# One hybrid S5 / attention / SSD step: attention of each head pair woven with the next pair's products, modulation of layer 0 on TensorE

## The chip, the cores and the metric

The kernel runs on one core of one Trainium2 chip. The metric is device time in microseconds (us) from one launch to its end. TensorE (PE) multiplies, VectorE (DVE), ScalarE (ACT) and GpSimd (POOL) work element by element, SyncE (SP) issues almost all transfers. Each engine takes its own instructions in order.

## The reference

Two trunk layers run over 512 latent tokens and 128 context tokens, 1024 channels each, in float32. The change touches layer 0 only. What it computes:

```
sh, sc, gt, shf, scf, gtf = split(silu(cond) @ ada_w + ada_b, 6)     # for c and for c_ctx
h    = rmsnorm(x) * (1 + sc) + sh
proj = h @ w_in                              # 1024 -> 512 (S5 input) + 512 q + 512 k + 512 v
y_s5 = s5(proj[:512]);  y_s5 = gelu(y_s5) * sigmoid(gelu(y_s5) @ w_glu)
       # bidirectional linear recurrence, 32 groups of 16 channels, 64 complex states
attn = 8 heads of 64; latent queries see an 8 x 16 window with a bias table plus 128 cached
       keys in one softmax, context queries see the context
x    = x + gt * (concat(y_s5, attn) @ w_out)
x    = x + gtf * swiglu(rmsnorm(x) * (1 + scf) + shf)
```

The keys and values of the context tokens and the final S5 states are outputs too. Layer 1 (a Mamba-2 mixer and its feed-forward part) follows, and a last norm.

## The kernel before

**Layout and products.** Channels lie on the 128 partitions, the 640 tokens along the free dimension. A product with float32 weights is done in three passes: weights and inputs are each split into a high and a low part of type fp32r (`split`: ScalarE copies the high part, VectorE subtracts), and TensorE sums hi x hi, hi x lo, lo x hi. `gemm` (line 294) does 8 x 3 x 2 = 48 matmuls of 320 columns for one 128-wide output tile. The mixer's input projection has 16 such products: m = 0 to 3 give the S5 input `uT`, and for each head pair p the products 4 + p, 8 + p and 12 + p give q, k and v (`qkv`, three steps of a generator).

**Order.** Instructions are written by Python generators that yield between steps; a driver takes steps of several of them in turn ("weaves" them). The order of the text is a priority; a planner with a cost model of its own then fixes the order on each engine, allots the buffers and puts in the waits. `behind(engine)` keeps what a block holds behind the last instruction of that engine. Buffers come from an arena of 12 blocks (`blk`, 10 KB a partition) and 2 large ones (`big`); weights have 3 slots each for `whi` and `wlo`, 2 for `wraw`. PSUM has 4 one-bank tiles (`pm`) and 2 two-bank tiles (`acc`).

**Modulation.** One of layer 0's 48 modulation tiles (128 outputs, two conditions) is computed in one of two ways. `ada_rows` streams the weights through TensorE with the condition as a stationary operand of 2 columns, 512 outputs a matmul, and transposes the row back. `ada_tile` (line 248) has the weights transposed in DRAM and lets VectorE multiply and sum them with the condition spread over all partitions, one instruction for each of the two conditions. At the start, `ada_rows` makes tiles 0 to 11 (shift, first half of scale) and `ada_tile` tiles 12 to 15. Tiles 24 to 28 come in the S5 stage (`adae`), 29 to 39 in `ada_fill` during the later q, k, v products and attention, 16 to 23 in the output projection (`ada`), 40 to 47 and layer 1 in the feed-forward part.

**S5.** Input and output maps are built from the parameters (`s5_params`, `s5_input_maps`, `s5_output_maps`) by VectorE, GpSimd and TensorE. `s5_scan` runs 63 steps: backward on GpSimd, forward on VectorE (`mt`, `s5x`). The first 16 steps have four operations, the others three, each needing the one before. `s5_out` then makes the outputs in four blocks, and `glu` four products.

**Attention of a pair** (`attention(p)`, 13 steps) works on five query blocks: scores on TensorE, bias and row minimum in one VectorE reduction (line 1267), Exp on ScalarE, reciprocal and scaling on VectorE (line 1271), transposes (line 1278), products with the values (line 1291) into one `acc` tile that is held to the end.

**The order around the change.** `even_mixer` does all four pairs' q, k, v first, with four scan steps to each product; pairs 0 to 2 are written to DRAM (`qd`). Then attention(3) is woven with the rest of the scan; `qkv_back` reads a pair back before its attention; attention(0) has modulation tiles and the first steps of `s5_out`, attention(1) and (2) the rest of `s5_out` and `glu`. Each attention writes its output split into `ah`, `al`. The output projection (`ev_w_out`, eight products) follows in `build`, each with one modulation tile, the residual and the next norm's tile.

Of the kernel before, what the change touches and what calls it, by code (L numbers as in the profile page):

```python
# [16 lines left out]
NS, NP = 512, 128  # L17
# [47 lines left out]
def lay_out(a):  # L65
# [9 lines left out]
    d["ada_w"] = np.ascontiguousarray(a["ada_w"].transpose(0, 2, 1).reshape(96, 128, 1024)[12:])  # L75
# [45 lines left out]
class Kernel:  # L121
# [43 lines left out]
    def load_consts(self):  # L165
        self.nc.sync.dma_start(self.ident, self.I["ident"])
        self.nc.sync.dma_start(self.vecs, self.I["vecs"])
        self.condf = self.const.tile([128, 8, 2], F32, name="condf")
        self.nc.sync.dma_start(self.condf, self.I["cond_f"])
        self.nc.scalar.activation(self.condf, self.condf, AF.Silu)  # L170
# [18 lines left out]
    def load_cond(self):  # L189
        nc = self.nc  # L190
        self.condr = self.blk("condr", [BLK])[:1]
        nc.sync.dma_start(self.condr[:, :2048], self.I["cond"])
        nc.vector.memset(self.condr[:, 2048:2176], 1.0)

    def spread_cond(self):
        nc = self.nc
        self.cond = self.blk("cond", [2, 1024])
        cond = self.cond.rearrange("p s n -> p (s n)")
        for i in range(4):
            ps = self.psum()  # L200
            nc.tensor.matmul(ps, self.condr[:, 2048:2176], self.condr[:, i * 512:i * 512 + 512], start=True, stop=True)
            with self.behind(nc.scalar):
                nc.scalar.activation(cond[:, i * 512:i * 512 + 512], ps, AF.Silu)

    def ada_stage(self):
        nc, I = self.nc, self.I
        slot = lambda n: self.wpool.tile([128, 8, 128], F32, name=n, **({"bufs": 2} if n == "wraw" else {})).rearrange("p k m -> p (k m)")
        def rows(src, o, tiles):
            for i, b in enumerate(tiles):
                for j in range(0, 4, 1):  # L210
                    nc.sync.dma_start(b[:, j:j + 1], I[src][4 * i + j:4 * i + j + 1, :, o:o + 512].rearrange("k p n -> p k n"))
            return [b[:, j] for b in tiles for j in range(4)]

        self.sck = rows("ada_sc", 0, [self.blk("adak", [4, 512]) for _ in range(2)])
        self.scw = [slot("whi" if i % 2 else "wlo") for i in range(4)]
        for i in range(4):
            nc.sync.dma_start(self.scw[i], I["ada_w"][i])
        self.shk = rows("ada_sh", 0, [self.blk("adak", [4, 512]) for _ in range(2)])
        large = self.big("adab", [8, 512])
        self.w0 = self.raw_w(I["ev_w_in"][0], 8)  # L220
        self.shl = rows("ada_sh", 512, [large[:, :4], large[:, 4:]])

    def ada_rows(self, w, at):
        nc = self.nc
        n = w[0].shape[-1] // 512
        acc = self.mm.tile([128, 2, 512], F32, name="acc")
        ps = [acc[:, h] for h in range(n)]
        for k in range(8):
            for h in range(n):
                nc.tensor.matmul(ps[h][:2], self.condf[:, k], w[k][:, h * 512:h * 512 + 512], start=k == 0, stop=k == 7)  # L230
            yield
        row = self.blk("adar", [1024])[:2]
        for h in range(n):
            nc.scalar.activation(row[:, h * 512:h * 512 + 512], ps[h][:2], AF.Copy)
        pt = self.psum()
        for j in range(4 * n):
            nc.tensor.transpose(pt[:, 2 * j:2 * j + 2], row[:, j * 128:j * 128 + 128], self.ident[:2, :2])
        b = self.vec("ada_b")[:, at:at + 4 * n]
        nc.vector.tensor_tensor(self.mod[0][:, at:at + 4 * n], pt[:, :8 * n].rearrange("p (k s) -> p k s", s=2),
                                b[:, :, None].to_broadcast([128, 4 * n, 2]), op=OP.add)  # L240
        yield
# [9 lines left out]
    def ada(self, layer, tiles):  # L251
        nc = self.nc
        for j in tiles:
            w = self.adar[:, self.adai % 5]
            self.adai += 1
            nc.sync.dma_start(w, self.I["ada_w"][layer * 48 + j - 12])
            self.ada_tile(layer, j, w)
            if j < 24 and layer == 0:
                self.ada_bias(0, j, j + 1)
            elif j % 8 == 7:  # L260
# [877 lines left out]
    def mixer_input(self):  # L1138
# [8 lines left out]
        self.spread_cond()  # L1147
        scale, shift, shift2 = self.ada_rows(self.sck, 8), self.ada_rows(self.shk, 0), self.ada_rows(self.shl, 4)
        for _ in range(0):
            next(scale)  # L1150
# [7 lines left out]
        for i, (sc, sf) in enumerate(((scale, shift), (self.scw, shift2))):  # L1158
            q = slice(4 * i, 4 * i + 4)
            if i:  # L1160
                for j in range(4):
                    self.ada_tile(0, 12 + j, sc[j])
                self.ada_bias(0, 12, 16)
            else:
                for _ in sc:
                    pass
            nc.vector.scalar_tensor_tensor(am[:, q], sh[:, 8 + 4 * i:12 + 4 * i], 1.0, g[:, q, None].to_broadcast([128, 4, 2]),
                                           op0=OP.add, op1=OP.mult)
            for k in range(4 * i, 4 * i + 4):
                xk = self.x[:, k]  # L1170
                self.tt(nc.gpsimd if k % 2 else nc.vector, xk, xk, r, OP.mult)
                for s, (a, b, _) in enumerate(SEGS):
                    nc.scalar.activation(xk[:, a:b], xk[:, a:b], AF.Copy, scale=am[:, k, s:s + 1])
            for _ in sf:
                pass
            for k in range(4 * i, 4 * i + 4):
                xh, xl = self.xt(k)
                for s, (a, b, _) in enumerate(SEGS):
                    nc.scalar.activation(xh[:, a:b], self.x[:, k, a:b], AF.Identity, bias=sh[:, k, s:s + 1])  # L1179
                    nc.vector.scalar_tensor_tensor(xl[:, a:b], self.x[:, k, a:b], sh[:, k, s:s + 1], xh[:, a:b].bitcast(F32),  # L1180
                                                   op0=OP.add, op1=OP.subtract)
# [5 lines left out]
    def qkv(self, p):  # L1187
# [3 lines left out]
        for n in range(3):  # L1191
# [9 lines left out]
            if p < 3:  # L1201
                nc.sync.dma_start(self.qd[p][:, n], o)
            yield

    def qkv_back(self, p):
        b = self.blk("qkvb", [3, T])
        self.nc.sync.dma_start(b, self.qd[p])
        self.qkvt[p] = [b[:, n] for n in range(3)]

    def ada_fill(self):  # L1210
        nc = self.nc
# [269 lines left out]
```

## Time and profile before

| | us |
|---|---|
| median of 3 runs | 1979.69 (1977.22 to 1979.78) |
| the profiled execution | 1977.53 |
| its span, first to last instruction | 1975.5 |
| TensorE busy in the span | 1883.6 (95%) |
| VectorE busy | 1332.7 (67%) |
| ScalarE busy | 744.8 (38%) |
| GpSimd busy | 452.7 (23%) |
| mean granted TensorE clock | 0.971 of full speed |

A group of the profile names line, engine, operation, the tiles written and read (out<-in), the shape, and how often it ran; busy time and the mean duration of one follow, then the idle time of the engine just ahead and what ended it. A float32 matmul that isn't split stands as two records. Busy time of TensorE includes the pipelined end of a matmul, so it is not work at its peak. The granted clock is the share of full speed that TensorE was given.

### The profile page before, as it was taken

Reading aid. Unit: us, or ns where it says so; the run is one execution under the profiler, and the core shown is the slowest. Engines: PE = TensorE matmul, PEld = TensorE weight load, DVE = VectorE, ACT = ScalarE, POOL = GpSimd, SP = SyncE. Lnnn points to the kernel's source line nnn. Section 1 sums busy time; section 2 is a strip of 40 time slices with the busy share of each in tenths; the row PEclk is TensorE's granted clock in tenths of the full one; section 3 lists DMA queues with packets and bytes.
Section 4 is the critical chain, followed back from the end, with each engine's and each line's share of the span. In section 5 each row is a group of like instructions: output and inputs, shape, how many; then the busy total and the mean of one; then the engine's idle time right before and its main releaser. Section 6 shows DMA issues by size and latency. Waiting matters only on the chain.

```text
span 1975.5 us, 30783 instructions
## 1 busy us (share of the span) xinstructions
PE 1883.6 (95%) x12364; PEld 1753.4 (89%) x12364; DVE 1332.7 (67%) x2210; ACT 744.8 (38%) x1235; POOL 452.7 (23%) x451
## 2 busy tenths in 40 slices
PE   7959779999999999999999999998999999999997
PEld 2859748899999999999998788875999999999997
DVE  7999996697855865876778696879555343443444
ACT  5444245543222222234555565655433221221222
POOL 2648860020000000002023444356441000000002
PEclk9979879999999999999999999998999999999999
DMA  7437455544533443533221213133412222222212
GB/s 285 147 106 213 150 178 150 188 151 151 173 107 119 158 133 120 164 101 99 90 76 49 86 49 96 60 96 89 163 65 75 75 75 75 75 68 83 75 58 82
DMA packets 104879, 224.85 MB, mean 114 GB/s; under 512 B 15377, under 2 KB 50849, under 8 KB 103841
## 3 DMA queue, kind: packets, MB, share of 16 engines
q1 hardware_dynamic: 104706, 222.88, 35.0%
q8 instruction: 97, 1.59, 0.3%
q14 instruction: 44, 0.36, 0.1%
q0 software_dynamic: 32, 0.02, 0.0%
HBM read 197.37 MB, written 22.84 MB: 111 GB/s over the span
## 4 chain that ended last, share of the span: by engine, by line
PE 78%; DVE 8%; ACT 1%; issue 1%; DMA 0%; POOL 0%; SPq 0%; DVEq 0%; ACTq 0%
PE acc L294 66%; PE pm L697 1%; PE pm L630 1%; PE pm L457 1%; PE pm L712 1%; PE acc L457 1%; PE acc L1291 1%; PE pm L1096 1%; DVE s5x L181 1%; DVE ssdw L686 1%; DVE junk L248 1%; PE pm L679 1%; DVE cv L563 1%; DVE wlo L186 1%; PE pm L1278 1%
## 5 line engine op out<-in xcount | busy, mean ns | idle before, releaser
L294 PE MATMUL acc<-xh,wlo 128*128 128x322 f32 (+2 forms) x2320 | 547.9, 317 | 10.6 <-DVE wlo L186 10.6
L294 PE MATMUL acc<-xh,whi 128*128 128x322 f32 (+2 forms) x2320 | 550.3, 317 | 7.7 <-ACT xh L1179 4.9
L294 PE MATMUL acc<-xl,whi 128*128 128x322 f32 (+2 forms) x2320 | 547.4, 315 | 0.0
L185 ACT ACTIVATE whi<-wraw 128x1024 fp32r<-128x1024 f32 (+2 forms) x212 | 221.0, 1043 | 682.3 <-PE acc L294 442.9
L294 PEld LDWEIGHTS acc<-xh,whi 128*128 128x128 f32 (+1 forms) x2320 | 395.5, 190 | 20.4 <-issue 10.1
L294 PEld LDWEIGHTS acc<-xh,wlo 128*128 128x128 f32 (+1 forms) x2320 | 393.0, 190 | 21.7 <-DVE wlo L186 11.6
L294 PEld LDWEIGHTS acc<-xl,whi 128*128 128x128 f32 (+1 forms) x2320 | 395.0, 190 | 8.3 <-issue 7.8
L181 POOL TENSOR_TENSOR ssq<-ssq 128x640 f32<-128x640 f32 (+2 forms) x45 | 72.6, 1614 | 1104.0 <-ACT ssq L328 511.7
L186 DVE TENSOR_TENSOR wlo<-wraw,whi 128x1024 fp32r<-128x1024 f32 (+2 forms) x212 | 263.3, 1242 | 25.4 <-ACT whi L185 24.2
L370 DVE TENSOR_TENSOR ffw<-acc,rext 128x644 f32<-128x644 f32 x88 | 72.9, 828 | 202.7 <-PE acc L294 198.5
L248 DVE CUSTOM_DVE_ANT_0 junk<-adar,cond 128x1024 bf16<-128x1024 f32 x128 | 156.2, 1220 | 1.8
L385 DVE SCALAR_TENSOR_TENSOR x<-acc,mod,x 128x320 f32<-128x320 f32 x144 | 54.4, 433 | 146.0 <-PE acc L294 146.0
L294 PE MATMUL acc<-hh,wlo 128*128 128x320 f32 x592 | 134.5, 309 | 0.0
L294 PE MATMUL acc<-hl,whi 128*128 128x320 f32 x592 | 134.4, 308 | 0.0
L294 PE MATMUL acc<-hh,whi 128*128 128x320 f32 x592 | 134.4, 309 | 0.0
L563 DVE SCALAR_TENSOR_TENSOR cv<-cv,vecs 128x644 f32<-128x644 f32 x96 | 98.0, 1021 | 14.6 <-ACT cv L561 13.0
L294 PEld LDWEIGHTS acc<-hl,whi 128*128 128x128 f32 x592 | 98.9, 188 | 0.0
L294 PEld LDWEIGHTS acc<-hh,wlo 128*128 128x128 f32 x592 | 98.8, 188 | 0.0
L294 PEld LDWEIGHTS acc<-hh,whi 128*128 128x128 f32 x592 | 98.8, 188 | 0.0
L185 ACT ACTIVATE hh<-ffw 128x640 fp32r<-128x640 f32 x44 | 32.5, 739 | 95.4 <-DVE ffw L418 95.4
L686 DVE SCALAR_TENSOR_TENSOR ssdw<-ssdw,dtk,ssdcb 128x128 f32<-128x128 f32 x160 | 60.6, 441 | 10.5 <-ACT ssdw L684 10.2
L181 POOL TENSOR_TENSOR ssds<-ssds,dtk 128x512 f32<-128x512 f32 x24 | 31.1, 1296 | 152.9 <-PE pm L697 89.9
(359 smaller groups left out, 2883.6 us busy)
## 6 DMA issues: line engine op xcount, KB each, us to landing
adar<-in_ada_w SPq DMA_DIRECT2D x64, 512.0 KB, 3.9
wraw<-in_ffn_w_gate SPq DMA_DIRECT2D x44, 512.0 KB, 3.3
wraw<-in_ffn_w_up SPq DMA_DIRECT2D x44, 512.0 KB, 3.3
wraw<-in_od_w_in SPq DMA_DIRECT2D x40, 512.0 KB, 3.3
wraw<-in_ffn_w_down SPq DMA_DIRECT2D x32, 448.0 KB, 3.3
wraw<-in_ev_w_in SPq DMA_DIRECT2D x16, 512.0 KB, 4.0
wraw<-in_ffn_w_down SPq DMA_DIRECT2D x16, 512.0 KB, 3.6
wraw<-in_od_w_out SPq DMA_DIRECT2D x16, 512.0 KB, 3.7
```

What stands on the lines that cost most here:

```text
L181: e.tensor_tensor(o, a, b, op=op)
L185: self.nc.scalar.activation(hi, x, AF.Copy)
L186: self.nc.vector.tensor_tensor(lo, x, hi.bitcast(F32), op=OP.subtract)
L248: nc.vector.tensor_tensor_reduce(out=junk, in0=w, in1=self.cond[:, s], scale=1.0, scalar=0.0, op0=OP.mult, op1=OP.add, accum_out=self.mod[ ...
L294: nc.tensor.matmul(ps[:mw, h, :n], a[:, k, :mw], b[:, h * n:(h + 1) * n], start=k0 + k == 0 and q == 0, stop=k0 + k == total - 1 and q == 2)
L370: self.nc.vector.tensor_tensor(t.rearrange("p (h n) -> p h n", h=2), ps[:, :, :GH], self.rext.rearrange("p (h n) -> p h n", h=2), op=OP.mult)
L385: nc.vector.scalar_tensor_tensor(xk[:, a:b], pv, gate[:, m, s:s + 1], xk[:, a:b], op0=OP.mult, op1=OP.add)
L457: nc.tensor.matmul(ps[:, :n], w[:, k], x[:, a:b], start=k == 0 and q == 0, stop=k == nf - 1 and q == 2)
L563: nc.vector.scalar_tensor_tensor(acc, cb[:, k:k + G], cw[:, k * 24 + wi:k * 24 + wi + 1], acc, op0=OP.mult, op1=OP.add)
L630: nc.tensor.matmul(ps, Bt[:, c], xw, start=True, stop=True)
L679: nc.tensor.matmul(ps, LH[r], RH[r, hf * 4:hf * 4 + 4].rearrange("p h l -> p (h l)"), start=True, stop=True)
L686: nc.vector.scalar_tensor_tensor(E[:, h], E[:, h], self.dt[:, 0, c, g * 8 + h:g * 8 + h + 1], cbs, op0=OP.mult, op1=OP.mult)
```

## The change

Layer 0's tiles 0 to 39 all go to TensorE, in five units of 1024 outputs (`ada_unit`): unit 1 (scale) and unit 0 (shift) at the start, units 2, 3 and 4 (gate, and the feed-forward part's shift and scale) in the last attention. A unit holds one PSUM bank: four groups of 32 partitions, two for the halves of the 1024 outputs and two for the even and odd blocks of the sum, so that each of the 16 matmuls has 32 stationary columns (the two conditions, and zeros). One copy, four transposes and two additions give the tiles. Units 2 to 4 read their weights, two rows of 512 KB at a time, into the two parts of one block.

The condition spread over the partitions is no longer made by TensorE and kept in DRAM; it is laid out by the host and loaded before the output projection. The q, k, v of a pair stay in their block; attention(p) for p = 0, 1, 2 is woven with the three products of pair p + 1 (at steps 1, 5 and 9) and one or two scan steps a step; attention(3) has the splits of the earlier pairs' output, the modulation units, and `s5_out` and `glu` from its third step on. The rest of `s5_out` and `glu` comes after it. Attention writes its output unsplit into one tile `af`.

```diff
-    d["ada_sc"] = np.ascontiguousarray(w[:, :, 1024:1536])
-    d["ada_sh"] = np.ascontiguousarray(w[:, :, :1024])
-    d["cond"] = np.ascontiguousarray(np.concatenate([a["c"][0], a["c_ctx"]])[None])
+    d["ada_n"] = np.ascontiguousarray(w[:, :, :5120].reshape(8, 128, 5, 1024).transpose(2, 0, 1, 3))
+    d["cond"] = np.ascontiguousarray(np.broadcast_to(np.stack([a["c"][0], a["c_ctx"]])[None], (128, 2, 1024)))
...
     def load_cond(self):
+        self.cond = self.blk("cond", [2, 1024])
+        self.nc.sync.dma_start(self.cond, self.I["cond"])
+        self.nc.scalar.activation(self.cond, self.cond, AF.Silu)
+
+    def ada_stage(self):
+        nc = self.nc
+        slot = lambda n: self.wpool.tile([128, 8, 128], F32, name=n).rearrange("p k m -> p (k m)")
+        self.scw = [slot("whi" if i % 2 else "wlo") for i in range(6)]
+        def two():
+            b = self.blk("adak", [BLK])
+            self.adrow.append(b[:, 2048:2560])
+            return [b[:, 0:1024], b[:, 1024:2048]]
...
+        for w, u in ((self.scw, 1), (self.shw, 0)):
+            for k in range(8):
+                if k == len(w):
+                    w += two()
+                nc.sync.dma_start(w[k], self.I["ada_n"][u, k])
+            if u:
+                self.w0 = self.raw_w(self.I["ev_w_in"][0], 8)
+
+    def ada_unit(self, u, pair, row):
+        nc = self.nc
+        ps = self.psum()
+        for i in range(4):
+            w = pair(i)
+            for a in range(2):
+                for b in range(2):
+                    q = 32 * (2 * a + b)
+                    nc.tensor.matmul(ps[q:q + 32], self.condf[:, 2 * i + a], w[a][:, b * 512:b * 512 + 512], start=i == 0, stop=i == 3)
+            if i < 3:
+                yield
+        nc.scalar.activation(row, ps, AF.Copy)
+        pt = self.psum()
+        for j in range(4):
+            nc.tensor.transpose(pt[:, j * 128:j * 128 + 128], row[:, j * 128:j * 128 + 128], self.ident)
...
+        nc.vector.tensor_tensor(m, part[:, 0, :, :, :2], v[:, :, :, None].to_broadcast([128, 2, 4, 2]), op=OP.add)
+        nc.vector.tensor_tensor(m, part[:, 1, :, :, :2], m, op=OP.add)
         yield
...
     def mixer_input(self):
...
+        for _ in self.ada_unit(1, pairs(self.scw), self.adrow[0]):
+            pass
         r = self.rext[:, :T]
         self.rstd(1024, r[:, :NS], r[:, NS:])
...
+        for k in range(8):
+            xk = self.x[:, k]
+            self.tt(nc.gpsimd if k % 2 else nc.vector, xk, xk, r, OP.mult)
...
+        for _ in self.ada_unit(0, pairs(self.shw), self.adrow[1]):
+            pass
...
     def ada_fill(self):
+        blk = self.blk("adaw", [BLK])
+
+        def pair(u):
+            def of(i):
+                w = [blk[:, a * 1024:a * 1024 + 1024] for a in range(2)]
+                for a in range(2):
+                    self.nc.sync.dma_start(w[a], self.I["ada_n"][u, 2 * i + a])
+                return w
+            return of
+
+        for u in (2, 3, 4):
+            yield from self.ada_unit(u, pair(u), blk[:, 2048:2560])
...
     def attention(self, p):
...
+        o = self.af[:, p]
+        nc.scalar.activation(o[:, :NS].rearrange("p (r w) -> p w r", r=8), pvs[:, 0].rearrange("p (w r) -> p w r", r=8), AF.Copy)
+        nc.scalar.activation(o[:, NS:], pvs[:, 1, :128], AF.Copy)
...
     def even_mixer(self):
...
-        with self.behind(nc.vector):
-            b = self.big("adae", [5, 1024])
...
-                self.ada_tile(0, 24 + i, b[:, i % 3])
...
         bg = self.s5_scan(0)
+        self.weave2(self.qkv(0), (bg, 4))
...
+        self.load_bias(0)
+        for p in range(3):
+            nxt = self.qkv(p + 1)
+            for i, _ in enumerate(self.attention(p)):
+                if i in (1, 5, 9):
+                    next(nxt)
+                if i == 8:
+                    self.load_bias(p + 1)
+                for _ in range(1 + (i % 3 == 2)):
+                    next(bg, None)
         for _ in bg:
             pass
+        ah, al = self.blk("ah", [4, T], F32R), self.blk("al", [4, T], F32R)
+        fill = self.ada_fill()
         out = chain(self.s5_out(), self.glu())
+        for i, _ in enumerate(self.attention(3)):
+            if i < 3:
+                self.split(ah[:, i], al[:, i], af[:, i])
+            next(fill, None)
+            if i > 1:
                 next(out, None)
...
+        for _ in fill:
+            pass
+        self.split(ah[:, 3], al[:, 3], af[:, 3])
         for _ in out:
             pass
...
         for m in range(8):
             w = K.load_w(I["ev_w_out"][m], 8)
             ps = K.gemm(w, kt, 8, TH)
-            K.ada(0, range(16 + m, 17 + m))
             K.residual(K.xk(m), ps, m, gate)
```

## Rows read from the trace of the kernel before

**Rows 1.** By stretches: length, busy (instructions) by engine, clock, DMA share, GB/s.
```profile
0.00:46.00 46.00, 33.70 (x89) 9.90 (x89) 35.31 (x99) 24.69 (x42) 13.45 (x11) 0.99 0.85 306
46.00:130.00 84.00, 64.65 (x428) 61.45 (x428) 76.60 (x92) 34.67 (x71) 49.60 (x20) 0.82 0.41 137
130.00:170.00 40.00, 32.81 (x286) 30.82 (x290) 36.50 (x28) 22.11 (x41) 22.33 (x16) 0.87 0.56 137
170.00:298.00 128.00, 104.30 (x640) 90.10 (x640) 119.95 (x320) 37.99 (x100) 98.82 (x194) 0.84 0.54 176
298.00:386.00 88.00, 85.27 (x651) 71.45 (x645) 55.11 (x156) 51.60 (x137) 0.00 (x0) 1.00 0.55 178
386.00:447.00 61.00, 60.32 (x398) 59.84 (x399) 53.60 (x97) 22.58 (x35) 13.45 (x6) 0.97 0.42 139
447.00:1975.50 1528.50, 1502.57 (x9885) 1429.87 (x9884) 955.65 (x1421) 551.14 (x814) 255.09 (x206) 0.99 0.30 96
```

**Rows 2.** Timeline, TensorE, start-up: start, length, instruction, count, [idle before].
```profile
39.30 1.88 PE L230 MATMUL acc<-adab,condf 128*2 128x512 f32 x4
46.04 0.93 PE L294 MATMUL acc<-xh,whi 128*128 128x320 f32 x2 [4.86 <-ACT xh L1179]
```

**Rows 3.** Timeline of ScalarE, start-up.
```profile
41.65 3.73 ACT L1173 ACTIVATE x<-x,amul 128x512 f32<-128x512 f32 x8 [2.98 <-DVE amul L1167]
45.28 3.72 ACT L1179 ACTIVATE xh<-x,mod 128x512 fp32r<-128x512 f32 x8
```

**Rows 4.** Timeline of VectorE, S5 maps.
```profile
92.91 3.17 DVE L248 CUSTOM_DVE_ANT_0 junk<-adae 128x1024 bf16<-128x1024 f32 x1
...
117.07 1.21 DVE L248 CUSTOM_DVE_ANT_0 junk<-adae 128x1024 bf16<-128x1024 f32 x1
...
130.62 1.95 DVE L181 TENSOR_TENSOR s5bp<-s5f,s5f 128x1024 f32<-128x1024 f32 x1 [3.08 <-DMA kd<-s5f]
```

**Rows 5.** Timeline of GpSimd, S5 maps.
```profile
104.23 10.69 POOL L181 TENSOR_TENSOR s5f<-s5f 128x1152 f32<-128x1152 f32 x3
```

**Rows 6.** VectorE's groups, 170 to 298 us: busy, mean ns, idle before, releaser.
```profile
L248 DVE CUSTOM_DVE_ANT_0 cond<-wlo,cond 128x1024 bf16<-128x1024 f32 x9 | 11.0, 1227 | 0.0
L248 DVE CUSTOM_DVE_ANT_0 cond<-whi,cond 128x1024 bf16<-128x1024 f32 x8 | 9.8, 1228 | 0.0
...
L1267 DVE CUSTOM_DVE_ANT_0 attw<-pm,rpb 128x384 f32<-128x384 f32 (+2 forms) x17 | 8.3, 489 | 4.1 <-PE pm L1264 4.1
L1271 DVE TENSOR_SCALAR attw<-attw,rc 128x384 f32<-128x384 f32 (+2 forms) x16 | 6.2, 393 | 0.0
```

**Rows 7.** VectorE by shape, 202 to 220 us, then 264 to 298 us.
```profile
L181 DVE TENSOR_TENSOR s5x<-s5x,mt 128x64 f32<-128x64 f32 x23 | 9.2, 400 | 0.8
L181 DVE TENSOR_TENSOR mt<-s5x,s5co 128x128 f32<-128x128 f32 x12 | 5.1, 423 | 0.4
...
L181 DVE TENSOR_TENSOR s5x<-s5x,mt 128x64 f32<-128x64 f32 x30 | 9.2, 308 | 0.4
L181 DVE TENSOR_TENSOR mt<-s5x,s5co 128x128 f32<-128x128 f32 x15 | 5.3, 356 | 0.1
```

**Rows 8.** TensorE at line 294, one projection product, columns as in rows 1.
```profile
161.10:168.50 7.40, 7.35 (x48) 7.09 (x48) 1.00 0.99 226
```

**Rows 9.** TensorE at lines 294 and 1291, 298 to 386 us.
```profile
298.00:386.00 88.00, 22.79 (x135) 19.75 (x135) 1.00 0.55 178
...
298.00:386.00 88.00, 13.94 (x138) 8.11 (x132) 1.00 0.55 178
```

**Rows 10.** Timeline of TensorE, S5 output.
```profile
299.65 0.38 PE L1094 MATMUL pm<-wraw,s5u 128*81 128x128 f32 x2
...
300.43 0.38 PE L1094 MATMUL pm<-wraw,s5u 128*81 128x128 f32 x2
```

**Rows 11.** DMA issues: count, KB each, median us to landing.
```profile
wlo<-in_ada_w SPq DMA_DIRECT2D x8, 512.0 KB, 5.1
```

**Rows 12.** Timeline of TensorE, products of 32 columns.
```profile
120.51 1.52 PE L988 MATMUL pm<-s5f,s5f 128*32 128x128 f32 x48
```

More of the change, by code (lines that the diff above doesn't have):

```diff
@@ L167, in load_consts @@
         self.nc.sync.dma_start(self.vecs, self.I["vecs"])
-        self.condf = self.const.tile([128, 8, 2], F32, name="condf")
-        self.nc.sync.dma_start(self.condf, self.I["cond_f"])
-        self.nc.scalar.activation(self.condf, self.condf, AF.Silu)
+        cf = self.small.tile([128, 8, 2], F32, name="condr", bufs=1)
+        self.nc.sync.dma_start(cf, self.I["cond_f"])
+        self.condf = self.const.tile([128, 8, 32], F32, name="condf")
+        self.nc.vector.memset(self.condf, 0.0)
+        self.nc.scalar.activation(self.condf[:, :, :2], cf, AF.Silu)
         self.s5s = self.blk("s5s", [40, 64])
@@ L196, in spread_cond @@
+    def ada_unit(self, u, pair, row):
         nc = self.nc
-        self.cond = self.blk("cond", [2, 1024])
-        cond = self.cond.rearrange("p s n -> p (s n)")
+        ps = self.psum()
         for i in range(4):
[L200 to L234, printed above, removed]
-        pt = self.psum()
[L236 to L240, printed above, removed]
+            w = pair(i)
@@ L1146, in mixer_input @@
         self.ssq = b[:, 0:2]
[L1147 to L1150, printed above, removed]
+        pairs = lambda w: lambda i: w[2 * i:2 * i + 2]
+        for _ in self.ada_unit(1, pairs(self.scw), self.adrow[0]):
+            pass
         r = self.rext[:, :T]
@@ L1331, in even_mixer @@
             nc.scalar.activation(uT[:, m, NS + 8:], ps[:, 1, 192:320], AF.Copy)
-        with self.behind(nc.vector):
-            b = self.big("adae", [5, 1024])
-            self.cond = b[:, 3:5]
-            nc.sync.dma_start(self.cond, cd)
-            for i in range(5):
-                nc.sync.dma_start(b[:, i % 3], self.I["ada_w"][12 + i])
-                self.ada_tile(0, 24 + i, b[:, i % 3])
         for _ in self.s5_chunks(uT):
@@ L1349, in even_mixer @@
         bg = self.s5_scan(0)
-        for p in range(4):
-            if p == 2:
-                cb = self.blk("cond", [BLK])
-                self.cond = cb[:, :2048].rearrange("p (s n) -> p s n", s=2)
-                self.junk2 = cb[:, 2048:2560].bitcast(BF16)
-                nc.sync.dma_start(self.cond, cd)
-                fill = self.ada_fill()
-            self.weave2(self.qkv(p) if p else first, (bg, 4), *([(islice(fill, 3), 1)] if p >= 2 else []))
+        self.weave2(self.qkv(0), (bg, 4))
         aw = self.blk("attw", [BLK])
@@ L1396, in even_mixer @@
                 nc.sync.dma_start(self.wglu.rearrange("p m k n -> p m (k n)"), self.I["s5_w_glu"].rearrange("m p x -> p m x"))
-        for i, _ in enumerate(self.attention(2)):
-            for _ in range(2):
-                next(out, None)
+        for _ in fill:
+            pass
+        self.split(ah[:, 3], al[:, 3], af[:, 3])
         for _ in out:
@@ L1410, in build @@
         K.load_consts()
-        K.load_cond()
         K.load_x()
```

108 lines of the change are left out of this document (22 added, 86 removed).

## Prediction

> **What bounds the kernel now.** I read the busy time by stretches first, to see which engine is full where [rows 1]. The reader is to see five stages before 447 us and one after it. From 0 to 46 us transfers fill the modulation weights in (DMA share 0.85). From 46 to 170 us, where the S5 maps are built, VectorE is busy 113 us of 124 and TensorE waits for it. From 170 to 298 us VectorE is busy 120 of 128 us: this is the forward scan. From 298 to 386 us TensorE is busy 85 of 88 us. From 386 to 447 us, the output projection, TensorE is busy 60.3 of 61. All that follows takes 1528.5 us, with TensorE busy 98%. So the change meets two stages that VectorE bounds and two that TensorE bounds; what VectorE is spared counts only in the first two. Then I read the order of the first 46 us [rows 2, 3], the VectorE and GpSimd order around 100 us [rows 4, 5], the groups of VectorE in the scan stage [rows 6, 7], and TensorE's groups around and after it [rows 8 to 10].
>
> **The parts of the change and their sum.** The durations are those of the profiled execution: 1977.53 us, of which 1975.5 us are span and 2.0 us lie around it; the median of the three runs shown is 2.2 us above it. I sum against 1977.5.
>
> *Start-up.* The same 8 MB of modulation weights come in, but 4 MB of scale first, then 4 MB of shift. Before, four of the scale tiles were eight VectorE reductions, and the second half of the scale was known only after 40 us: ScalarE scales the second half of x from 41.65 us and writes xh from 45.28 us [rows 3], so that the first projection starts at 46.04 us [rows 2]. After, ScalarE can scale all of x while the shift is still coming. What is late then is the shift. Before, TensorE passes 24 modulation products one behind the other, at 0.94 us each (four records in 1.88 us, two a product), until 41.2 us [rows 2]; after, only the last four products wait for the last transfers. The transfers keep the DMA busy for 0.85 x 46 = 39 us in all, a few of them not the modulation's, so the last lands at 37 to 38 us; products, a copy, four transposes and two additions take about 3 us more, and the first xh follows at once. First projection at about 41 us: -5 us (0 to -8). VectorE, for which the next stage waits, also loses the eight reductions (8 x 1.2 = 10 us of its 35 [rows 1]) and gets xh in one run instead of two. I take -7 us for the next stage's start.
>
> *The five modulation tiles in the S5 stage.* Ten reductions go from VectorE. Three run beside GpSimd's work and take 3.2 us, the other seven 1.2 us [rows 4], 18 us in all. Between 117 and 127 us seven of them share the queue with two weight splits and small work, and the next maps wait at 130.62 us for a transfer that depends on that small work [rows 4]. GpSimd ends its last output map at 114.9 us [rows 5]; TensorE's 1.5 us on it [rows 12], copies, small work and the write to DRAM follow, some 11 us with the 3.1 us of waiting at the end. If GpSimd's end doesn't move, only 130.6 - 114.9 - 11.7 = 4 us come back; if VectorE alone is the gate, all 18. I take -10 us (-4 to -18), since both bind in turn. The Trainium skill (SBUF — State Buffer, section "SBUF: two separate sides") has VectorE with two SBUF inputs and GpSimd take a shared port pair as an exclusive lock, the loser waiting out the winner's instruction. The 3.2 us beside GpSimd against 1.2 us after it agree. By that rule the three removed reductions also bring GpSimd's end 3 x 1.2 = 3.7 us forward, and with GpSimd as the gate this term would be -8 us.
>
> *Scan stage.* Before, it holds the products of three pairs, attention of pair 3 and some of pair 0. After, it holds the products of pairs 1 to 3 and attention of pairs 0 to 2. VectorE: 17 reductions go, 11.0 + 9.8 = 21 us. Its attention groups were 17 of the 40 score tiles, 8.3 + 6.2 = 14.5 us [rows 6]; for 30 tiles that is 25.6 us, +11, and +2 for their reciprocals. Two more weight splits, 1.2 us each, +2.5 us. A scan step costs 0.423 + 2 x 0.400 = 1.22 us where only the scan runs, and 0.356 + 2 x 0.308 = 0.97 us where attention lies between its operations [rows 7]; about 32 more steps are woven so, -8 us. VectorE's sum is 120 - 21 + 13 + 2.5 - 8 = 106 us. TensorE: nine products of 7.35 us [rows 8] are 66 us, and three attentions of 13 us (next paragraph) 39 us, together 105 us. Two engines with 105 us each that wait for one another will not run gapless; before, 8 us were lost with one of them full. I allow 20 us and take 126 us against 128: -2 us. The ends are 108 us (nothing lost) and 153 us (each of the nine products holds the scan up by 3 us).
>
> *The stage after the scan.* TensorE's 85.3 us are 22.8 us of products [rows 9]; the S5 output, 32 groups of six records at a pitch of 0.78 us, 25 us [rows 10], and its 32 short transposes, about 3 us at that pitch; the remaining 34.5 us are attention. 138 records of line 1291 lie here [rows 9], 52 make a pair (26 products in the code), so 2.65 pairs, 13 us each. After, 1 pair is left: 85.3 - 1.65 x 13 = 64 us. Three modulation units come in. One is 16 products of 128x512, 32 records. In line four such records take 1.88 us [rows 2], a unit 15 us. But the unit writes four groups of 32 columns, and line 988, which does that, passes 48 records of 128 columns in 1.52 us [rows 12]: scaled to 512 columns 0.127 us a record, 4.1 us a unit. I take that row, as it has the same form: 3 x 4.1 = 12.3 us (12 to 45). Sum 76.5 us, and 2.7 us of idle time as before: 79 us against 88, -9 us. Less attention is left to hide the S5 output chain and the GLU; that is in the upper end (+10 us). The split of the collected attention (four pairs of operations of about 0.8 us) hides under TensorE.
>
> *Output projection.* 16 reductions (16 x 1.2 = 19 us of VectorE) go from a stage in which TensorE is busy 60.3 of 61 us: it starts and ends a little sooner, -2 us (0 to -4). The 1 MB condition tile is loaded and passed through Silu here on ScalarE; nothing needs it before the feed-forward part.
>
> *Spills.* Nine writes and three reads of products are gone. They were on no wait of an engine that I read; removing them is 0 in time. It frees the sync queue, worth 0 to -2 us. What pays for it is arena space: in the scan stage xh, xl, the S5 input, two pairs' products, two bias tiles and the three attention tiles make exactly the 12 blocks, so nothing can be fetched further ahead.
>
> Sum: -7 - 10 - 2 - 9 - 2 = -30 us, 1977.5 - 30 = 1947.5, about 1948 us.
>
> **Rivals.**
> *The weave starves the scan.* VectorE takes its queue in order; a score reduction placed before scan steps waits if TensorE is in a 7.35 us product. For it: score reductions already wait 4.1 us for TensorE in the scan stage [rows 6]. Against: the planner places scan steps where it expects the wait. At 3 us for each of nine products the scan stage takes 27 us more: 1948 + 27 = 1975 us, about no change.
> *The modulation chain stalls TensorE (slower).* In the last attention the three units are fed through one pair of buffers: the next pair of 512 KB transfers can't start before the four products of the last one have read it. Twelve pairs, each 5.1 us from issue to landing where such tiles go beside other transfers [rows 11] and about 1 us of products. If the planner puts the products into TensorE's order earlier than the data comes, TensorE stands with the S5 output and the GLU behind it. At 4.2 us a pair that is 50 us: 1998 us. It decides the sign from 30 / 12 = 2.5 us a pair on. Against: ready work of the S5 output can be ordered between, and only the output projection's norm needs units 3 and 4.
> *Better overlap.* If both engines stay full in the scan stage (108 us), and all of the ten reductions come back (-18 us), it is 1948 - 18 - 8 = 1922 us; with the other terms at their ends 1916. For it: the granted clock was 0.84 over the scan stage [rows 1], so TensorE spent a third of it at the lower of its two levels, 1.2 instead of 2.4 GHz, with attention and few products; more products between keep it at work.
> *The weave isn't made.* The order on each engine is the planner's; it may leave attention and products in blocks. Then the two middle stages keep 128 and 88 us, the units' 12 us come on top of a full TensorE, and only the other parts remain: 1977.5 - 7 - 10 - 2 + 12 = 1970.5 us.
>
> **Chances and range.** Forecast (1948, own range 1928 to 1968): 0.57. Weave not made: 0.05. Better overlap: 0.13. Starved scan: 0.13. Modulation chain: 0.12. 0.2% is about what a measurement of this kernel can tell from no change, here 4 us around 1979.7. Faster: the first three and a third of the starved case, 0.79; the same 0.08; slower 0.13 (the chain and a tail of the starved case). The range that leaves out 2 in 10 goes from the better case's centre to the starved one's far side: 1916 to 1979 us.
>
> **What would show it.** In the trace after: the first projection at 40 to 42 us; the forward scan starting at about 153 us on VectorE, ending at about 279; VectorE and TensorE both over 80% in between, with the granted clock above 0.84; the stage from there to the first output projection about 79 us; line-for-line durations of the products unchanged; the last 1528 us unchanged to 3 us. The records of the modulation units should start in groups of four. Wrong would be: TensorE waiting for transfers of modulation weights by more than 10 us in all, or the scan ending after 295 us.

## The result and the profile after

The changed kernel takes 1998.55 us (median of 4 runs, 1998.31 to 2003.32), the kernel before 1978.94 us in runs beside it: ratio 1.0106, 95% interval 1.0088 to 1.0123. It is 20 us slower; 1948 us was forecast, with 1916 to 1979 as the range. The profiled execution took 1998.31 us, of which 1996.3 us are span, 20.8 us more than before.

The first view of after is the busy time by stretches, with columns as in [rows 1], cut at the first projection, where VectorE's last maps and the scan start, at the scan's end, at the first product of the output projection (it reads kh, the split S5 output), and in the feed-forward part.

```profile
0.00:45.00 45.00, 19.66 (x97) 6.13 (x97) 26.70 (x86) 24.68 (x41) 13.32 (x11) 0.96 0.81 301
45.00:118.00 73.00, 60.18 (x400) 57.31 (x401) 60.77 (x69) 27.72 (x61) 47.80 (x19) 0.89 0.31 93
118.00:157.00 39.00, 34.31 (x287) 32.29 (x286) 36.22 (x28) 23.91 (x45) 22.09 (x14) 0.91 0.57 138
157.00:269.00 112.00, 99.01 (x679) 83.80 (x679) 103.73 (x324) 47.03 (x130) 86.80 (x196) 0.89 0.34 103
269.00:405.00 136.00, 114.16 (x705) 80.23 (x700) 38.58 (x104) 45.86 (x109) 0.00 (x0) 0.87 0.56 180
405.00:467.00 62.00, 61.97 (x422) 61.56 (x421) 39.51 (x62) 29.25 (x41) 11.79 (x6) 1.00 0.32 109
467.00:1996.30 1529.30, 1501.96 (x9901) 1431.81 (x9900) 957.38 (x1421) 551.21 (x814) 257.50 (x206) 0.99 0.30 96
```

Against [rows 1] the start-up is 1 us shorter, the S5 stage 12 us (124 to 112) and the scan stage 16 us (128 to 112). The stage after the scan is 48 us longer (88 to 136); the rest adds 2 us. One cut is not the same on both sides. [Rows 1] cuts at 386 us, but the kernel before had begun the output projection ahead of that, among its last attention; TensorE's timeline of before:

```profile
373.52 0.56 PE L294 MATMUL acc<-kh,whi 128*128 128x320 f32 x2
```

Up to 386 us, 39 of its records were done, 6 us at the 0.153 us a record of [rows 8]. So, like for like, the stage is 54 us longer, and what follows is 4 us shorter. Everything that is lost is lost in that one stage: its granted clock fell from 1.00 to 0.87, and TensorE is idle for 22 of its 136 us, where it was idle for 3 of 88.

Two lists of waits of after say for what, from 269 to 405 us: TensorE's first lines (PEld is its weight load), then SP's queue of transfers, from 240 to 420 us. The columns are the waiting line, what it waited for, us in total, times, the longest; adaw is the block that the rows of weights are loaded into.

```profile
PEld pm L224 <- DMA adaw<-in_ada_n: 22.7, 11, 3.6
PE pm L224 <- DMA adaw<-in_ada_n: 12.0, 9, 2.7
...
PE acc L287 <- ACT gh L186: 6.5, 2, 4.9
```

```profile
SPq L1192 <- PE pm L224: 25.0, 17, 2.9
SPq L1192 <- DMA adaw<-in_ada_n: 19.2, 10, 4.9
```

TensorE waits for modulation rows, and SP's queue, which is to load the next ones into the same block, waits for TensorE to have read the last. The timeline of TensorE in that stage shows how they alternate (start, length, instruction, count, [idle before]).

```profile
297.52 1.05 PE L224 MATMUL pm<-adaw,condf 128*32 128x512 f32 x4
...
301.87 1.05 PE L224 MATMUL pm<-adaw,condf 128*32 128x512 f32 x4 [0.92 <-DMA adaw<-in_ada_n]
304.64 1.92 PE L224 MATMUL pm<-adaw,condf 128*32 128x512 f32 x4 [1.72 <-DMA adaw<-in_ada_n]
307.23 1.92 PE L224 MATMUL pm<-adaw,condf 128*32 128x512 f32 x4 [0.67 <-DMA adaw<-in_ada_n]
309.99 1.92 PE L224 MATMUL pm<-adaw,condf 128*32 128x512 f32 x4 [0.84 <-DMA adaw<-in_ada_n]
312.61 1.12 PE L230 MATMUL pm<-ident,adaw 128*128 128x128 f32 x4 [0.70 <-ACT adaw L227]
313.52 0.63 PE L1087 MATMUL pm<-wraw,s5u 128*81 128x128 f32 x2
...
319.20 1.07 PE L224 MATMUL pm<-adaw,condf 128*32 128x512 f32 x8
```

The last two pairs of this unit (four groups of four records, one group a row) stand back to back in TensorE's order, and S5 output stands behind them (line 1087), the second half of a block whose first half ran from 293.91 us with the same maps. The second unit ends in the same way, from 330 to 341 us. After three of the gaps the four records (two products) take 1.92 us in place of 1.05: from 304.6 to 312 us the granted clock is 0.50, the lower of its two levels. A row that comes alone costs more, too: its four records take 1.05 us, as long as the eight of two rows together (1.07 us, the last line), as one row fills only two of the four groups. The chain of waits, from 255 to 420 us, puts the units on the path that sets the end; shares are of 165 us.

```profile
by line: PE acc L287 32.1%; DMA adaw<-in_ada_n 15.3%; PE pm L1089 11.6%; PE pm L224 10.9%; PE acc L1269 5.3%; PE pm L1087 5.1%; PE pm L1242 3.3%; PE pm L1256 3.2%; PE pm L1239 2.7%; PE pm L230 1.7%; PE pm L1098 1.4%; ACT adaw L227 1.1%; iss
```

Transfers 25 us, products 18, transposes 2.8 and copies 1.8: 48 us, about what the stage grew. That they lie on the chain doesn't yet show that the stage would be shorter without them; the experiments do.

### The profile page after: what moved, and what is told of

Same layout as the page of the kernel before. It is cut to its first block, busy times and chain, and to the rows that moved or that the text cites. A ratio compares the mean times of both kernels' runs of the same rounds, so it can differ in the third digit from the quotient of the medians.

```text
span 1996.3 us, 30838 instructions
## 1 busy us (share of the span) xinstructions
PE 1891.3 (95%) x12476; PEld 1753.1 (88%) x12476; DVE 1262.9 (63%) x2090; ACT 749.7 (38%) x1238; POOL 439.3 (22%) x451
## 4 chain that ended last, share of the span: by engine, by line
PE 81%; DVE 6%; ACT 2%; DMA 2%; issue 1%; SPq 0%; DVEq 0%; ACTq 0%
PE acc L287 69%; DMA adaw<-in_ada_n 1%; PE pm L450 1%; DVE s5x L182 1%; PE acc L450 1%; PE pm L623 1%; PE pm L690 1%; PE pm L705 1%; PE pm L1089 1%; PE pm L224 1%; DVE cv L556 1%; PE pm L672 1%; DVE mt L182 1%; DVE ssdw L679 1%; PE acc L1269 1%
## 5 line engine op out<-in xcount | busy, mean ns | idle before, releaser
L287 PEld LDWEIGHTS acc<-xl,whi 128*128 128x128 f32 (+1 forms) x2320 | 396.6, 191 | 12.3 <-issue 9.6
L187 DVE TENSOR_TENSOR wlo<-wraw,whi 128x1024 fp32r<-128x1024 f32 (+2 forms) x212 | 268.8, 1268 | 29.8 <-ACT whi L186 28.4
L243 DVE CUSTOM_DVE_ANT_0 junk<-adar,cond 128x1024 bf16<-128x1024 f32 x112 | 136.8, 1221 | 1.8
L287 PE MATMUL acc<-yl,whi 128*128 128x320 f32 x256 | 61.6, 321 | 5.9 <-DVE yl L761 5.9
```

The costliest lines, as they stand in the source:

```text
L187: self.nc.vector.tensor_tensor(lo, x, hi.bitcast(F32), op=OP.subtract)
L243: nc.vector.tensor_tensor_reduce(out=junk, in0=w, in1=self.cond[:, s], scale=1.0, scalar=0.0, op0=OP.mult, op1=OP.add, accum_out=self.mod[ ...
L287: nc.tensor.matmul(ps[:mw, h, :n], a[:, k, :mw], b[:, h * n:(h + 1) * n], start=k0 + k == 0 and q == 0, stop=k0 + k == total - 1 and q == 2)
```

## The experiments

All times are medians, and each ratio is to runs of the kernel before on the same chip, with its 95% interval. The stage after the scan goes from the scan's end to the first product of kh. Line numbers are those of each kernel's own file.

**No units.**

```
     def ada_fill(self):
-        blk = self.blk("adaw", [BLK])
...
+        self.nc.vector.memset(self.mod[0][:, 16:40], 0.125)
+        yield
```

> Left out: the modulation units 2 to 4 (tiles 16 to 39), whose values are replaced by a constant, so the output is not the reference's. Theory 1 (the three units' transfer chain, standing in TensorE's order among the attention, is what cost the time after the scan): the stretch from the scan's end to the first matmul of the output projection, 136 us in the changed kernel, falls to about 85 to 90, and the kernel takes about 1950 us, 48 less. Rival A (woven attention leaves nothing to cover the S5 output and the GLU, so the stretch stays long without the units too): the stretch stays over 115 us and the kernel over 1975.

1953.35 us, ratio 0.9875 (0.986 to 0.989); the stage after the scan is 86.0 us, from 270.5 to the first product of kh at 356.5, by the columns of [rows 1]:

```profile
270.50:356.50 86.00, 81.09 (x599) 72.02 (x598) 38.77 (x101) 44.57 (x108) 0.00 (x0) 0.96 0.46 140
```

Rival A falls: the three units cost 46 us (1.0106 - 0.9875 of 1978).

**One load.** The units' work stays, the transfers go.

```
                 for a in range(2):
-                    self.nc.sync.dma_start(w[a], self.I["ada_n"][u, 2 * i + a])
+                    if u == 2 and i == 0:
+                        self.nc.sync.dma_start(w[a], self.I["ada_n"][u, 2 * i + a])
```

> Left out: all loads of the units 2 to 4 but the first pair's, so the matmuls run on stale blocks and the output is not the reference's; every matmul, transpose and addition of the units stays. Theory 1 (waiting for transfers): the waits of TensorE for adaw go, the stretch after the scan falls to about 100 us and the kernel takes 1955 to 1965 us, at most 15 us more than the one with no units. Rival B (the units' own matmuls, transposes and evictions in TensorE's order cost the time, at the lower clock): the stretch stays over 120 us and the kernel over 1980.

1963.03 us, ratio 0.9925 (0.991 to 0.994). Waits for adaw are gone. The stage, and in it the 96 records of line 224 alone, by the columns of [rows 1] and then with TensorE's alone, followed by those records in the changed kernel:

```profile
269.20:366.60 97.40, 92.53 (x707) 74.39 (x706) 39.24 (x105) 46.01 (x110) 0.00 (x0) 0.98 0.42 130
```

```profile
269.20:366.60 97.40, 12.58 (x96) 0.98 0.42 130
...
269.00:405.00 136.00, 27.42 (x96) 0.87 0.56 180
```

It is 11.4 us longer than with no units, and the products take 12.58 us (27.42 in the changed kernel). So the work costs 11 us and the transfers 39 us (136.0 - 97.4), 36 by the ratios, 3 us a pair. Not all of the 39 us is idle time. By the views, TensorE is idle for 17 us more, line 224 takes 15 us more, and the other records 7 us more, at the lower clock. Of the 15 us, some 8 go to rows that come one at a time and some 6 to the lower clock, estimated from the timeline's groups. Rival B falls.

**Three blocks, and its control.** The control has the late split, with one block.

```
-        blk = self.blk("adaw", [BLK])
+        blks = [self.blk("adaw", [BLK]) for _ in range(3)]
...
+                b = blks[(4 * u + i) % 3]
...
-            if i < 3:
-                self.split(ah[:, i], al[:, i], af[:, i])
...
-        self.split(ah[:, 3], al[:, 3], af[:, 3])
+        for i in range(4):
+            self.split(ah[:, i], al[:, i], af[:, i])
```

> Nothing is left out: the units 2 to 4 load into three blocks in turn instead of one, so six rows are under way instead of two; in return the four pairs' split into ah and al comes after the attention. Theory 1a (the stretch is short of transfer time: 12.6 MB have to come in after the scan whatever the number of blocks): at the 315 GB/s that the units reached in the run with early units they take 40 us instead of 48, so 1985 to 1993 us. Theory 1b (the round trip of one block, load, multiply, load again, is what costs): with loads ahead of use TensorE's waits for adaw fall under 5 us and the kernel takes 1970 us or less.

> Nothing is left out: the control of the run with three blocks. One block as in the changed kernel, but the four pairs' split into ah and al after the attention, as there. Theory 1b (the round trip through one block costs): the stall stays, 1992 to 2003 us. Rival (the later split, not the number of blocks, won those 29 us): 1980 us or less.

Three blocks take 1969.43 us, ratio 0.996 (0.9946 to 0.9974); the control 1996.14 us, 1.0092 (1.0071 to 1.0114). So it is the blocks, 26 us by the ratios, and theory 1a, that the stage is short of transfer time, falls. The stage with three blocks, and then its transfers and those of the changed kernel (count, KB each, median us from issue to landing):

```profile
268.10:375.00 106.90, 100.71 (x720) 78.41 (x719) 39.35 (x106) 46.41 (x111) 0.00 (x0) 0.96 0.67 229
```

```profile
adaw<-in_ada_n SPq DMA_DIRECT2D x24, 512.0 KB, 6.0
```

```profile
adaw<-in_ada_n SPq DMA_DIRECT2D x24, 512.0 KB, 3.9
```

With six rows under way one transfer takes longer, 6.0 us for 3.9, yet all of them come sooner: 229 GB/s in the stage for 180. What had cost was the round trip through one block. TensorE no longer waits for adaw at all. That is 26 of the 36 us; the stage is still 9.5 us longer than with one load (106.9 and 97.4), and no run shows why.

**Early units.** The units go into the S5 map stage, through a large tile with room for two pairs.

```
-        blk = self.blk("adaw", [BLK])
+        b = self.big("adae", [5, 1024])
...
         for m in range(0, 4):
+            for _ in range(3):
+                next(fill)
```

> Nothing is left out: units 2 to 4 run in the S5 map stage, before the scan, out of a large tile that is free there. Theory 1: TensorE has idle time and the DMA queues are little used there, so the units delay the scan by less than 6 us, the stretch after the scan falls to 85 to 90 us, and the kernel takes 1945 to 1958 us. Rival C (the same chain of loads stalls TensorE wherever it stands, as it issues in order): the scan starts 15 us later or more, and the kernel takes 1970 us or more.

1983.20 us, ratio 1.003 (1.0017 to 1.0042): my theory fell, and rival C's numbers came. The scan starts at 194.4 us instead of 157.0. TensorE's timeline (first and last units):

```profile
113.05 1.90 PE L224 MATMUL pm<-adae,condf 128*32 128x512 f32 x16
117.64 1.05 PE L224 MATMUL pm<-adae,condf 128*32 128x512 f32 x4 [1.60 <-DMA adae<-in_ada_n]
121.48 4.48 PE L224 MATMUL pm<-adae,condf 128*32 128x512 f32 x12 [2.79 <-DMA adae<-in_ada_n]
...
147.96 4.01 PE L224 MATMUL pm<-adae,condf 128*32 128x512 f32 x12 [0.22 <-DMA adae<-in_ada_n]
```

The planner gathered the units again, into 39 us (113 to 152) in which TensorE had only six records of a projection besides, and the S5 transposes stood behind them. From 110 to 155 us the transfers run at 274 GB/s with a share of 0.79, nearly as in the start-up (301 and 0.81); there, too, TensorE waits for them. Idle TensorE time alone was no cover. Rival C's "wherever it stands" goes too far, as the units beside the scan show below. The stage after the scan is 86.1 us.

**The weave alone.** Tiles 16 to 39 on VectorE as before, 24 to 39 of them after the scan.

```
-        for u in (2, 3, 4):
-            yield from self.ada_unit(u, pair(u), blk[:, 2048:2560])
+        for j in range(24, 40):
+            w = slot(j)
+            nc.sync.dma_start(w, self.I["ada_w"][j - 16])
+            with self.behind(nc.vector):
+                self.ada_tile(0, j, w, junk)
+            yield
```

> Nothing is left out: the attention is woven as in the changed kernel, but the tiles 16 to 39 are formed on VectorE as before the change (tiles 24 to 39 in the stretch after the scan, 16 to 23 in the output projection). Theory 1 (the weave is a gain and the units are the loss): VectorE has room after the scan, about 48 us of tiles beside 90 us of S5 output, and the kernel takes 1950 to 1965 us. Rival A (the weave itself gives back after the scan what it wins before): 1975 us or more, with the stretch after the scan over 110 us.

1983.35 us, ratio 1.0023 (1.0013 to 1.0034): nearly rival A's numbers, but not for its reason. The stage after the scan is 109.5 us. The tiles' rows take the slots whi and wlo, which the S5 output needs too, and TensorE waits for its maps (its list of waits from 269 to 380 us):

```profile
PE pm L1091 <- DMA whi<-fd: 9.0, 2, 7.4
PE pm L1089 <- DMA wraw<-kd: 4.7, 1, 4.7
```

So the modulation is dear after the scan on VectorE too; that the weave itself is no loss, the next run shows.

**Neither tiles nor weave.** The kernel before without tiles 16 to 39, for the weave's own worth.

```
     def ada_fill(self):
...
+        self.nc.vector.memset(self.mod[0][:, 16:40], 0.125)
...
-            K.ada(0, range(16 + m, 17 + m))
```

> The kernel before, with the modulation tiles 16 to 39 left out (a constant in their place, so the output is not the reference's): with the changed kernel without its units, 1953 us, it gives the worth of the weave where no modulation work stands beside it. Theory 1 (the weave by itself is a gain): 1961 us or more, so 8 us or more for the weave and the other edits. Rival A (the weave gives nothing, all that the units' removal wins would be won without it): 1950 to 1957 us.

1962.59 us, ratio 0.9926 (0.9904 to 0.9947). Against 0.9875 the weave, with the start-up edits, is worth about 10 us where no modulation work is about.

**Units without the weave.** The order of before, units through weight slots beside the scan.

```
+        held = [load(*seq.pop(0))]
+        def pair(i):
+            if seq:
+                held.append(load(*seq.pop(0)))
+            return held.pop(0)
```

> Nothing is left out: the attention's order of the kernel before, with spills, but the tiles 16 to 39 as three TensorE units through the weight slots, stepped where the kernel before formed its tiles (last two head pairs' products, attention of pair 3 and of pair 0). Theory 1 (the units are no loss where their loads stand beside the scan): 1965 to 1975 us, with the scan starting at about 157 us of the span instead of 170. Rival C (the units stall TensorE in any order): 1985 us or more.

1970.68 us, ratio 0.9969 (0.9958 to 0.9979), as theory 1 has it; the scan starts at 161.6 us, 5 us later than expected.

**Weave and units in the scan.** The same slots, with the weave: a step at four of the thirteen places in each of the first three pairs' attention.

```
         for p in range(3):
...
+                if i in (0, 3, 7, 11):
+                    next(fill, None)
```

> Nothing is left out: the units 2 to 4 go through the weight slots whi and wlo, four steps beside each of the first three head pairs, so in the scan stage, one pair of rows loaded ahead. Theory 1 (only the transfers' place is wrong; the DMA queues have a share of 0.17 in the scan stage): the scan ends at most 12 us later (by 281 us of the span), the stretch after it falls to 85 to 92 us, and the kernel takes 1955 to 1970 us. Rival D (the slots are taken from the input products' weights, TensorE waits for those, and VectorE's scan waits for the products): the scan ends after 295 us and the kernel takes 1975 us or more.

1958.42 us, ratio 0.9903 (0.9884 to 0.9923). It is the fastest complete kernel of the study, 1.0% under the kernel before and 2.0% under the changed one. Scan stage and stage after it:

```profile
154.00:267.30 113.30, 101.53 (x674) 75.13 (x675) 103.41 (x317) 42.34 (x117) 86.12 (x195) 0.92 0.50 165
267.30:365.00 97.70, 92.80 (x684) 80.91 (x683) 42.58 (x115) 50.76 (x123) 0.00 (x0) 0.97 0.54 164
```

The scan stage is 1 us longer than in the changed kernel, though its DMA share went from 0.34 to 0.50: there the transfers are covered. (The 0.17 of the expectation is the share from 200 to 250 us alone.) Of the units' 96 records, 16 still ran after the scan. The run changes two things, the place and the buffers (a pair is loaded ahead, through the weight slots); more buffers without the new place gave 26 us, the two together 40. What the place alone gives is not isolated.

**Units from the first pair on.**

```
-        self.weave2(self.qkv(0), (bg, 4))
+        fill = self.ada_fill()
+        self.weave2(self.qkv(0), (bg, 4), (fill, 1))
...
-                if i in (0, 3, 7, 11):
+                if i in (2, 6, 10):
```

> Nothing is left out: as the run with the units in the scan, but their steps begin beside the first pair's products (three steps there, three beside each of the next three pairs), as there the last three pairs of rows were multiplied only after the scan's end. Theory 1: no unit stands behind the scan, the stretch after it falls from 98 us to 86 to 90, and the kernel takes 1952 to 1957 us. Rival D (the work is only moved into the scan, which VectorE and TensorE fill): the scan ends 5 us later or more, and the time stays within 3 us of 1958.

1965.94 us, ratio 0.9938 (0.9923 to 0.9953): both expectations missed. The scan ended sooner, at 259.4 us, and the first product of kh came later, at 372.7 us for 365.0. The planner put more behind the scan: 270 records of products for 218, 120 of line 1275 (products with the values) for 104, and 32 of the units for 16, so that the condition of theory 1 wasn't met. Which cost of its made it do so stays open.

**Second weight split behind xh.** For the start-up.

```
+            if m == 1:
+                raw = self.raw_w(self.I["ev_w_in"][1], 8)
+                with self.behind(nc.scalar):
+                    w = self.split_w(raw, 8)
```

> Nothing is left out: as the run with the units in the scan, but the second product's weight split stands on ScalarE behind xh instead of ahead of it. If ScalarE's order holds the first projection back (copy of the modulation behind the x scaling, then two splits and a table load of 1.28 us ahead of xh), the first projection's first matmul comes 1 us earlier, 44 instead of 45.2, and the kernel takes 1955 to 1958 us. Rival: the second product then waits for its weights, and the time is 1958 us or more.

1963.08 us, ratio 0.9921 (0.9905 to 0.9938). The first projection starts at 43.42 us, as expected of ScalarE's order, but the time is no better (1958 without the edit): the products then wait for xl three times (3.7 us) instead of once (3.2 us), and the scan starts at 159.7 us for 153.9. By the ratios the two runs are 4 us apart, within their intervals.

The ratios side by side:

| | no tiles 16 to 39 | VectorE tiles | units after the scan | units in the scan |
|---|---|---|---|---|
| order of before | 0.9926 | 1 | - | 0.9969 |
| woven | 0.9875 | 1.0023 | 1.0106 | 0.9903 |

Woven, the modulation costs 6 us in the scan, 29 on VectorE after it, and 46 as the change has it; differences under 5 us are within the intervals.

## Why the prediction was wrong

**The step that failed** is the term of the stage after the scan: 88 to 79 us forecast, 136 measured. It counted three units as 12.3 us of TensorE and nothing for their transfers. The work was priced right: 12.58 us of records, 11.4 us of stage. Missing were the 39 us that the transfers cost, because TensorE's order stood at rows that had not come. My own sign of being wrong came: TensorE waited 12.0 us for them, where 10 was the limit. The rival of the modulation chain had the place, the mechanism and the sign, at 4.2 us a pair; 3 us was measured, so that its 1998 us is met only together with the other terms' misses, by luck. I gave it 0.12 because ready S5 output could be ordered between. For the last two pairs of two of the units it was not: the planner put them back to back. [Rows 11] had the transfer at 5.1 us, and with one block no load starts before the products on the last row are done. With 1 us of products, twelve pairs are a chain of 73 us, an estimate; it ran from 292 to 369 us, 77 us. In a stage forecast at 79 us that left no slack for an order that stands still at a wait, and it belonged into the sum.

The Trainium skill (Trainium Kernel Development and Optimization, section "Best Practices") asks for double buffering, to overlap transfers with compute. The trace agrees: one block against three is 26 us here.

**The same term, smaller:** without units the stage takes 86 us, not 66.7 (64 and 2.7 idle). The other 19 us are work that I had put into the scan stage, less some that left. The rows of after for TensorE at line 287 and at line 1269 (294 and 1291 before), columns as in [rows 9]:

```profile
269.00:405.10 136.10, 32.70 (x176) 0.87 0.56 180
...
269.00:405.10 136.10, 10.57 (x100) 0.87 0.56 180
```

Of the 176 records of products, 80 are input projections (they read xh and xl), 12 us at the 7.35 / 48 = 0.153 us of [rows 8]; of attention there are 48 records more than the 52 of the one pair planned, 0.9 x 13 = 12 us. Against that, I had read the 135 records of [rows 9] as work that stays, but 39 of them, 6 us, are the output projection's, and none of those lies ahead of the cut now. The 24 us came out of a scan stage that was 14 us shorter than forecast, so little of them is a loss.

**Start-up:** -7 forecast, -1 measured. The shift's products were done at 36.6 us, as the term has it; what it left out is ScalarE's order. Its timeline of after:

```profile
37.72 1.92 ACT L1155 ACTIVATE x<-x,amul 128x512 f32<-128x512 f32 x4 [0.16 <-DVE x L182]
39.54 0.57 ACT L227 ACTIVATE adak<-pm 128x512 f32<-128x512 f32 x1
40.02 1.04 ACT L186 ACTIVATE whi<-wraw 128x1024 fp32r<-128x1024 f32 x1
40.97 1.00 ACT L1155 ACTIVATE x<-x,amul 128x512 f32<-128x512 f32 x2
41.98 1.28 ACT L479 ACT_TABLE_LOAD   x1
43.28 0.20 ACT L479 ACTIVATE dtp<-dtp 64x1 f32<-64x1 f32 x1
43.39 1.04 ACT L186 ACTIVATE whi<-wraw 128x1024 fp32r<-128x1024 f32 x1
44.34 7.33 ACT L1161 ACTIVATE xh<-x,mod 128x512 fp32r<-128x512 f32 x16
```

The copy of the shift waits behind the scaling of x, and then a split, the rest of the scaling, a table load and another split stand ahead of xh. GpSimd's map work did start 6.6 us earlier (79.19 us for 85.79), as the term hoped for the next stage; but the scan starts only 2 us earlier than in the run with neither tiles nor weave (157.0 and 158.9 us), which has the old start-up.

**The five tiles:** -10 forecast (-4 to -18), right: -11 measured. The S5 stage is 12 us shorter, and the run with neither tiles nor weave isolates the tiles, as its code up to the scan differs from the kernel before in them alone. These rows show when VectorE's maps and GpSimd's group of [rows 5] start, in the kernel after and then in that run (before, 130.62 and 104.23 us):

```profile
118.05 1.22 DVE L182 TENSOR_TENSOR s5bp<-s5f,s5f 128x1024 f32<-128x1024 f32 x1
...
97.65 10.77 POOL L182 TENSOR_TENSOR s5f<-s5f 128x1152 f32<-128x1152 f32 x3
```

```profile
119.20 1.22 DVE L181 TENSOR_TENSOR s5bp<-s5f,s5f 128x1024 f32<-128x1024 f32 x1 [3.10 <-PE pm L1017]
...
104.49 9.81 POOL L181 TENSOR_TENSOR s5f<-s5f 128x1152 f32<-128x1152 f32 x3
```

Without the tiles the maps start 11 us earlier, while GpSimd ends only 0.6 us earlier (114.3 for 114.9 us). So the bound of 4 us, for a GpSimd whose end doesn't move, was wrong, and -10, taken between the two gates, came out right in part by luck. By the lock that the prediction cites, GpSimd's nine operations would end 3.7 us sooner without three reductions beside them; they took 28.3 us for 29.2. That is no clean test of the lock, since a weight split moved up beside them.

**Scan stage:** -2 forecast, -16 measured, for a start at 157 and an end at 269 us (153 and 279 forecast). VectorE's 103.7 us agree with the 106 of the sum; the 20 us allowed for mutual waits were too many, since work that didn't fit went behind the scan. VectorE is busy 93%, TensorE 88%, the clock 0.89. The starved scan didn't come.

**Output projection and rest:** -2 forecast, +2 measured, but -4 without the 6 us that only the cut puts there. **The weave isn't made:** it was; 114 records of line 1269, 2.2 pairs of heads, lie between 157 and 269 us.

**Spills at 0:** not isolated; the weave with all edits but the modulation after the scan is worth about 10 us.

## What to carry to other kernels

Moved weights bring their transfers along: price the chain load, multiply, load again by the number of blocks that are free at that place, before the arithmetic. Where one block is all there is, move the work to a stage where slots and transfers are to spare: the same units cost 46 us after the scan through one block, and 6 mostly beside the scan through the weight slots. A planner that orders by its own costs may gather what the code spreads, so look in the trace whether ready work really stands between the waits.

## What the runs showed of the hardware

The same 96 records of the units took 12.58 us of TensorE where no transfer was waited for and 27.42 us where one was, at granted clocks of 0.98 and 0.87 in the stage. Eight records that fill the four groups of 32 columns took 1.07 us, and four that fill two of them 1.05 us: half the groups, the same time. Two transfers of 512 KB under way landed in 3.9 us each, six in 6.0 us, and the stage moved 180 and 229 GB/s. The Trainium skill (TensorE: Matmul & The Clock Gate, section "HAM oscillation — how this bites in real kernels") has short runs of matmuls between waits for transfers start at the lower clock each time; the trace agrees in part, 1.92 us after some waits and 1.05 us after others.
